# The first two chunks of w_out, and the first gate and up chunk, advanced side by side up to their last quarter

## The chip, the cores and the metric
The kernel runs on one core of one Trainium2 chip. The time is device microseconds of one execution (us); a matmul runs on the tensor engine (PE), with its weight loads recorded as PEld; DVE is the vector engine, ACT the scalar engine, POOL is GpSimd, SP the engine that issues most DMAs.

## What is computed
One residual block over x of shape (1, 256, 2048) in float32: an mLSTM branch and an S5 branch run on one normed input and are merged by two gates; then come an output projection, a gated feed-forward layer, and a last norm. The part around the change is

```python
merged = g[..., 0, :] * y_m + g[..., 1, :] * y_s
x = x + merged @ w_out                                   # 2048 x 2048
h2 = rms_norm(x, norm_ffn_g)
x = x + (silu(h2 @ w_ffn_gate) * (h2 @ w_ffn_up)) @ w_ffn_down   # hidden size 5632
return rms_norm(x, norm_final_g)
```

## The kernel before
All weights stream through the core once, as one list `blocks` (built near its end) of 512 KB pieces: 256 rows (two row tiles, "kts") by 512 columns. A matrix of 2048 rows has eight such pieces, kp 0 to 7, for each chunk n of 512 columns; out0.6 is here the piece kp 6 of chunk 0 of `w_out`, fg0.6 and fu0.6 the same of `w_ffn_gate` and `w_ffn_up`. `w_out` has four chunks, gate and up eleven each, and their chunks alternate: gate 0, up 0, gate 1, up 1, and so on.

Each piece takes the same way. SP issues its DMA into `raw` (L144). ACT casts it to `hi` (L156, the high part in a format that the PE takes at full rate), DVE computes `lo = raw - hi` (the TT helper, L94), and `o2_block` issues 12 matmuls of 128 rows by 512 columns (2 row tiles x 2 halves of the 256 sequence rows x 3 products: hi x hi, lo x hi, hi x lo), recorded on the helper's line L100. `raw`, `hi` and `lo` have three buffers each. A new DMA can start when the `lo` of three pieces before is done, and a new cast when the PE has finished the piece three before. From gate 0 on, every piece whose index in the list leaves 3 when divided by 4 (L140) takes its `raw` from another pool of 8 KB buffers instead, and so doesn't wait for those three. The loop at the end emits the DMA of piece i+5 and the split of piece i+2 before the matmuls of piece i.

The left operands come in quarters. `turn` (L969) takes chunk n of the merged branches (after the last piece of chunk n of `w_up_m`), transposes it, sends it through DRAM on POOL's queue (`groups_dma`, L281 out into `bounce`, L283 back, four DMAs each), and casts it to `mTh`/`mTl` (L979). Chunk 3 of it feeds pieces kp 6 and 7 of every chunk of `w_out`. In the same way `out_mm` loads a 256 x 512 part of x at its first piece (L998), and after its last piece it adds the accumulators (L1003), takes the squares (L1005) and queues `x1_T`: two transposes on DVE into `x1sd` (L274), two 256 KB DMAs out and eight 64 KB DMAs back on POOL's queue, then four `h2h` on ACT (L1027) and four `h2l` on DVE (L1028). Chunk 3 of these feeds pieces kp 6 and 7 of every chunk of gate and up; chunk 2 feeds kp 4 and 5. After chunk 3, DVE and ACT also compute the norm's factor `r2` (L244, L245). Accumulators are two PSUM tiles for a chunk, from a ring of four.

The written order is not the order that runs: the instructions of each engine are put in order when the program is built, by a scheduler that plays the program through (`schedule_with_timeline_sim=True`, L1351). In the kernel before it already starts out1.0 between out0.5 and out0.6, and runs fu0.0 between fg0.5 and fg0.6.

Of the kernel before, what the change touches and what calls it, by code (L numbers as in the profile page):

```python
# [15 lines left out]
ADD, SUB, MUL, MAX, MIN = ALU.add, ALU.subtract, ALU.mult, ALU.max, ALU.min  # L16
# [31 lines left out]
def block_kernel(ctx: ExitStack, tc: tile.TileContext, d, out):  # L48
# [14 lines left out]
    def nm(s):  # L63
        uid[0] += 1
        return f"{s}_{uid[0]}"

    def u8(shape, dt=F32, name="u"):
        return up.tile(shape, dt, tag="u8", name=nm(name), bufs=NU8)

    def u16(shape, dt=F32, name="U"):  # L70
        return up.tile(shape, dt, tag="u16", name=nm(name), bufs=NU16)
# [4 lines left out]
    def t2(shape=(P, 512), dt=F32, name="t"):  # L76
        return tp.tile(list(shape), dt, tag="t2k", name=nm(name), bufs=NT2)
# [4 lines left out]
    def acc_tile():  # L82
        return pp.tile([P, 512], F32, tag="acc", name=nm("acc"), bufs=4)
# [9 lines left out]
    def TT(o, a, b, op):  # L93
        return V.tensor_tensor(o, a, b, op=op)  # L94
# [4 lines left out]
    def mm(o, l, r, start, stop):  # L99
        return PE.matmul(o, l, r, start=start, stop=stop, skip_group_check=True)  # L100
# [25 lines left out]
    blocks = []  # L126

    def add_mat(name, nchunk, nkp, fn_maker, order=None):
        for n in order if order is not None else range(nchunk):
            for kp in range(nkp):  # L130
                blocks.append((d[name][n, kp], fn_maker, (n, kp)))
# [28 lines left out]
    def o2_block(acc, lhs, kts, hi, lo, first, last):  # L160
        n = len(kts)
        for q, kt in enumerate(kts):
            h = hi[:, q * 512 : (q + 1) * 512]
            l = lo[:, q * 512 : (q + 1) * 512]
            for tt in range(2):
                xh, xl = lhs(kt, tt)
                mm(acc[tt], xh, h, first and q == 0, False)
                mm(acc[tt], xh, l, False, False)
                mm(acc[tt], xl, h, False, last and q == n - 1)

    def lhs_of(hts, lts, per):
        def g(kt, tt):
            a, b = divmod(kt, per)
            s = slice(tt * 128, (tt + 1) * 128)
            return hts[a][:, b, s], lts[a][:, b, s]
        return g
# [619 lines left out]
    cur = {}  # L796
# [191 lines left out]
    def out_mm(i, nk, hi, lo):  # L988
        n, kp = nk
        if n == 0 and kp == 0:  # L990
            cur["x1"] = u16([P, 2, 2048], name="x1")
            cur["h2h"] = [u8([P, 8, 256], F32R, name="h2h") for _ in range(2)]
            cur["h2l"] = [u8([P, 8, 256], F32R, name="h2l") for _ in range(2)]
        if kp == 0:
            cur["acc"] = [acc_tile(), acc_tile()]
            cs = slice(n * 512, n * 512 + 512)
            with tc.issue_after(wdma[0]):
                nc.sync.dma_start(cur["x1"][:, :, cs], d["x"].rearrange("(a p) c -> p a c", p=P)[:, :, cs])  # L998
        o2_block(cur["acc"], lhs_of(cur["mTh"], cur["mTl"], 8), (2 * kp, 2 * kp + 1), hi, lo, kp == 0, kp == 7)
        if kp == 7:  # L1000
            for tt in range(2):
                o = cur["x1"][:, tt, n * 512 : n * 512 + 512]
                TT(o, cur["acc"][tt], o, ADD)  # L1003
                jk = t2()
                A.activation(jk, o, AF.Square, accum_out=ss2[:, tt, n : n + 1])  # L1005
            later(lambda: x1_T(n))

    def x1_T(n):
        sd = u8([P, 2, 1024], name="x1sd")
        st_ = sd[:, 0].rearrange("p (t j a c) -> p t j a c", j=4, t=2, a=4)  # L1010
        for tt in range(2):
            blocks_T(st_[:, tt], cur["x1"][:, tt, n * 512 : n * 512 + 512])

        def move():
            for tt in range(2):
                groups_dma(
                    sd[:, 1].rearrange("p (t i x) -> p t i x", t=2, i=4)[:, tt],
                    sd[:, 0].rearrange("p (t j x) -> p t j x", j=4, t=2)[:, tt],
                )
            later(split)  # L1020

        def split():
            d_ = sd[:, 1].rearrange("p (t i a c) -> p a (t i) c", i=4, t=2, a=4)
            for a in range(4):
                ct = 4 * n + a
                v = lambda h: h[ct // 8][:, ct % 8, :].rearrange("p (i c) -> p i c", c=32)
                A.activation(v(cur["h2h"]), d_[:, a], AF.Copy, scale=pvs("g2", ct))  # L1027
                STT(v(cur["h2l"]), d_[:, a], pvs("g2", ct), f(v(cur["h2h"])), MUL, SUB)  # L1028

        later(move, 0)  # L1030
        if n == 3:
            s = cp.tile([P, 2], F32, name="ssum2")
            V.tensor_reduce(s, ss2, mybir.AxisListType.X, ADD)
            TS(s, s, 1.0 / D, EPS, MUL, ADD)
            rstd(r2, s, "r2")
# [15 lines left out]
    def ffn_mm(which):  # L1051
        def fn(i, nk, hi, lo):
            n, kp = nk
            if kp == 0:
                cur[which] = [acc_tile(), acc_tile()]
            o2_block(cur[which], lhs_of(cur["h2h"], cur["h2l"], 8), (2 * kp, 2 * kp + 1), hi, lo, kp == 0, kp == 7)
            if kp == 7 and which == "fg":
                cur["t1"] = []
                for tt in range(2):
                    sg, t1 = t2(), t2()  # L1060
                    A.activation(sg, cur["fg"][tt], AF.Sigmoid, scale=r2[:, tt : tt + 1])
                    STT(t1, cur["fg"][tt], r2[:, tt : tt + 1], sg, MUL, MUL)
                    cur["t1"].append(t1)
            if kp == 7 and which == "fu":
                hh, ll = a_tiles(n)
                for tt in range(2):
                    STT(cur["t1"][tt], cur["fu"][tt], r2[:, tt : tt + 1], cur["t1"][tt], MUL, MUL)
                    turn(n, tt, cur["t1"][tt], hh, ll)

        return fn  # L1070
# [83 lines left out]
        blocks.insert(len(blocks) - GLU, (d["w_glu"][0, b], glu_mm, (0, b)))  # L1154
    add_mat("w_up_s", 4, 2, ups_mm)
    add_mat("w_up_m", 4, 4, upm_mm)
    add_mat("w_out", 4, 8, out_mm)
    fg, fu = ffn_mm("fg"), ffn_mm("fu")
    FFN0 = len(blocks)
    for n in range(11):  # L1160
        for kp in range(8):
            blocks.append((d["w_ffn_gate"][n, kp], fg, (n, kp)))
        for kp in range(8):
            blocks.append((d["w_ffn_up"][n, kp], fu, (n, kp)))
    add_mat("w_ffn_down", 4, 22, down_mm)

    laters = []
# [1 line left out]
    def later(fn, delay=1):  # L1169
        laters.append([delay, fn])  # L1170
# [63 lines left out]
    for i in range(len(blocks)):  # L1234
# [24 lines left out]
        hi, lo = splits.pop(i)  # L1259
# [95 lines left out]
```

## Time and profile before

| | |
|---|---|
| median of three runs | 1260.47 us (1258.69 to 1264.71) |
| the profiled execution | 1258.85 us, of which its span is 1257.1 us |
| PE busy | 1233.7 us (98% of the span) |
| DVE, ACT, POOL busy | 803.8, 604.0, 106.6 us |
| mean granted PE clock | 0.995 of full speed |
| DMA, mean over the span | 205 GB/s |
| chain that ended last | PE 85%, DVE 6%, DMA 5%, issue 2%, ACT 1% |

The times in the rows below count from the start of the span. The chain of waits follows the work that ended last back to what released it, so that a piece of another engine in it marks a place where the PE stood still or was close to it. The granted clock of a window is a share of full speed; 1.0 is 2.4 GHz and 0.5 is 1.2 GHz.

### The profile page before, as it was taken

To read this page: it belongs to the slowest core of one execution; us is meant where nothing else is said; L and a number is where in the kernel's file an instruction comes from. 1 tells how busy PE (TensorE), PEld (TensorE's weight loads), DVE (VectorE), ACT (ScalarE), POOL (GpSimd) and SP (SyncE) were. 2 spreads that over 40 slices of the span, in tenths; PEclk is the share of its full clock that TensorE was granted. 3 is DMA by queue.
4 is the path that set the end of the run, shared out by engine and by line. 5 is a ranking of instruction groups with operands and counts; after the bars stand their busy time and mean duration, and the time that the engine had idled before them with its cause. 6 is when DMAs were issued, how large, how long until landed. Compare 5 with 4: busy or idle time off the path is not lost.

```text
span 1257.1 us, 15683 instructions
## 1 busy us (share of the span) xinstructions
PE 1233.7 (98%) x5738; PEld 1015.3 (81%) x5738; DVE 803.8 (64%) x1162; ACT 604.0 (48%) x752; POOL 106.6 (8%) x199
## 2 busy tenths in 40 slices
PE   7999999999999999989999999999999999999997
PEld 7777888887788878868888888888888888888885
DVE  8779945999877856645556555555555554554544
ACT  7574554446654445444344444434444443444433
POOL 0000000000000522211101100110111010000000
PEclk9999999999999999989999999999999999999999
DMA  7645655554555977877667766555765686666443
GB/s 265 208 137 178 194 184 182 167 160 143 190 182 193 280 265 256 286 239 224 217 203 228 222 212 217 187 184 204 245 228 183 225 279 198 196 198 199 152 161 141
DMA packets 75597, 258.19 MB, mean 205 GB/s; under 512 B 10496, under 2 KB 11264, under 8 KB 75520
## 3 DMA queue, kind: packets, MB, share of 16 engines
q1 hardware_dynamic: 67616, 237.25, 58.1%
q0 software_dynamic: 7904, 19.94, 4.8%
q8 instruction: 45, 0.74, 0.2%
q14 instruction: 32, 0.26, 0.1%
HBM read 245.09 MB, written 12.06 MB: 205 GB/s over the span
## 4 chain that ended last, share of the span: by engine, by line
PE 85%; DVE 6%; DMA 5%; issue 2%; ACT 1%; ACTq 0%; SPq 0%; DVEq 0%
PE acc L100 80%; PE aux L100 4%; DMA raw<-in_w_out_dram 4%; DVE lo L94 3%; ACT hi L156 1%; DMA raw<-in_w_ffn_gate_dram 1%; DVE xcT L97 1%; DVE stm L94 0%; DVE bu L94 0%; DMA raw<-in_w_up_m_dram 0%; DVE x L94 0%; DVE gm L94 0%; DMA raw<-in_w_in_dram 0%; PE aux L774 0%; DVE h2l L97 0%
## 5 line engine op out<-in xcount | busy, mean ns | idle before, releaser
L94 DVE TENSOR_TENSOR lo<-raw,hi 128x1024 fp32r<-128x1024 f32 x427 | 521.0, 1221 | 403.6 <-ACT hi L156 403.0
L156 ACT CAST hi<-raw 128x1024 fp32r<-128x1024 f32 x427 | 449.1, 1053 | 577.5 <-PE acc L100 488.9
L100 PE MATMUL acc<-lo,h2h 128*128 128x512 f32 x704 | 275.2, 391 | 0.6 <-DVE lo L94 0.5
L100 PE MATMUL acc<-hi,h2l 128*128 128x512 f32 x704 | 274.2, 390 | 0.0
L100 PE MATMUL acc<-hi,h2h 128*128 128x512 f32 x704 | 246.8, 391 | 4.2 <-ACT hi L156 4.2
L100 PE MATMUL acc<-hi,aT 128*128 128x512 f32 x664 | 204.6, 389 | 0.0
L100 PEld LDWEIGHTS acc<-hi,h2h 128*128 128x128 f32 x704 | 132.5, 189 | 32.7 <-ACT hi L156 5.3
L100 PEld LDWEIGHTS acc<-lo,h2h 128*128 128x128 f32 x704 | 132.7, 189 | 29.6 <-DVE lo L94 2.1
L100 PE MATMUL acc<-lo,hTh 128*128 128x512 f32 x384 | 153.6, 400 | 1.3 <-DVE lo L94 1.2
L100 PEld LDWEIGHTS acc<-hi,h2l 128*128 128x128 f32 x704 | 132.8, 189 | 27.4
L100 PE MATMUL acc<-hi,hTl 128*128 128x512 f32 x384 | 150.4, 392 | 0.0
L100 PEld LDWEIGHTS acc<-hi,aT 128*128 128x128 f32 x664 | 124.7, 188 | 25.9
L100 PE MATMUL acc<-hi,hTh 128*128 128x512 f32 x384 | 139.4, 393 | 0.0
L100 PE MATMUL acc<-lo,aT 128*128 128x512 f32 x332 | 129.1, 389 | 0.0
L100 PEld LDWEIGHTS acc<-lo,hTh 128*128 128x128 f32 x384 | 72.1, 188 | 22.1 <-DVE lo L94 4.0
L100 PEld LDWEIGHTS acc<-hi,hTh 128*128 128x128 f32 x384 | 71.7, 188 | 16.7 <-issue 2.0
L100 PEld LDWEIGHTS acc<-hi,hTl 128*128 128x128 f32 x384 | 72.2, 188 | 14.6 <-issue 0.7
L281 POOL DMA_DIRECT2D bounce<-m x30 | 16.9, 565 | 690.5 <-DVE m L274 690.2
L100 PEld LDWEIGHTS acc<-lo,aT 128*128 128x128 f32 x332 | 62.3, 188 | 12.9
L283 POOL DMA_DIRECT2D m<-bounce x120 | 65.6, 554 | 43.1 <-DMA bounce<-m 28.2
L100 PE MATMUL acc<-lo,mTh 128*128 128x512 f32 x128 | 50.0, 392 | 0.0
L100 PE MATMUL acc<-hi,mTl 128*128 128x512 f32 x128 | 49.5, 389 | 0.0
(246 smaller groups left out, 1077.7 us busy)
## 6 DMA issues: line engine op xcount, KB each, us to landing
raw<-in_w_in_dram SPq DMA_DIRECT2D x104, 512.0 KB, 3.5
raw<-in_w_ffn_gate_dram SPq DMA_DIRECT2D x88, 512.0 KB, 3.7
raw<-in_w_ffn_up_dram SPq DMA_DIRECT2D x88, 512.0 KB, 4.2
raw<-in_w_ffn_down_dram SPq DMA_DIRECT2D x88, 512.0 KB, 3.5
raw<-in_w_out_dram SPq DMA_DIRECT2D x32, 512.0 KB, 5.0
raw<-in_w_up_m_dram SPq DMA_DIRECT2D x16, 512.0 KB, 3.6
bounce<-m POOLq DMA_DIRECT2D x30, 256.0 KB, 4.1
m<-bounce POOLq DMA_DIRECT2D x120, 64.0 KB, 4.2
```

The lines of the kernel that those rows point to most:

```text
L94: return V.tensor_tensor(o, a, b, op=op)
L97: return V.scalar_tensor_tensor(out=o, in0=a, scalar=s, in1=b, op0=op0, op1=op1, **kw)
L100: return PE.matmul(o, l, r, start=start, stop=stop, skip_group_check=True)
L156: A.copy(hi, raw)
L281: nc.gpsimd.dma_start(bounce, st_)
L283: nc.gpsimd.dma_start(dt_[32 * j : 32 * j + 32], bounce.rearrange("(i r) j x -> r i j x", i=4)[:, :, j])
```

## The change
The list of pieces is put in another order at two places. Chunks 0 and 1 of `w_out` run as out0.0 to out0.5, out1.0 to out1.5, out0.6, out0.7, out1.6, out1.7; chunks 2 and 3 follow as they were. Gate 0 and up 0 run as fg0.0 to fg0.5, fu0.0 to fu0.5, fg0.6, fg0.7, fu0.6, fu0.7; all later chunks are as they were. So that two chunks of `w_out` can be open at once, their accumulators are kept under a key of their own. Nothing else is edited.

```diff
@@ -992,15 +992,15 @@
         if kp == 0:
-            cur["acc"] = [acc_tile(), acc_tile()]
+            cur["out", n] = [acc_tile(), acc_tile()]
...
-        o2_block(cur["acc"], lhs_of(cur["mTh"], cur["mTl"], 8), (2 * kp, 2 * kp + 1), hi, lo, kp == 0, kp == 7)
+        o2_block(cur["out", n], lhs_of(cur["mTh"], cur["mTl"], 8), (2 * kp, 2 * kp + 1), hi, lo, kp == 0, kp == 7)
...
-                TT(o, cur["acc"][tt], o, ADD)
+                TT(o, cur["out", n][tt], o, ADD)
@@ -1154,14 +1154,20 @@
-    add_mat("w_out", 4, 8, out_mm)
+
+    SPLIT = 6
+    for ms, a, b in (((0, 1), 0, SPLIT), ((0, 1), SPLIT, 8), ((2, 3), 0, 8)):
+        for m in ms:
+            for kp in range(a, b):
+                blocks.append((d["w_out"][m, kp], out_mm, (m, kp)))
     fg, fu = ffn_mm("fg"), ffn_mm("fu")
     FFN0 = len(blocks)
     for n in range(11):
-        for kp in range(8):
-            blocks.append((d["w_ffn_gate"][n, kp], fg, (n, kp)))
-        for kp in range(8):
-            blocks.append((d["w_ffn_up"][n, kp], fu, (n, kp)))
+        for a, b in ((0, SPLIT), (SPLIT, 8)) if n == 0 else ((0, 8),):
+            for kp in range(a, b):
+                blocks.append((d["w_ffn_gate"][n, kp], fg, (n, kp)))
+            for kp in range(a, b):
+                blocks.append((d["w_ffn_up"][n, kp], fu, (n, kp)))
```

The first place is on the PE where out0.5 ends. In the kernel before, `acc_4033` and `acc_4034` are chunk 0 and `acc_4204`, `acc_4205` chunk 1; `hi_4104` is out0.5, `hi_4122` out0.6, `hi_4158` out1.0.

```order
L100 MATMUL acc_4034<-lo_4105,mTh_3643 128x512
L100 MATMUL acc_4034<-hi_4104,mTl_3645 128x512
L100 MATMUL acc_4204<-hi_4158,mTh_3642 128x512
L100 MATMUL acc_4205<-hi_4158,mTh_3642 128x512
L100 MATMUL acc_4033<-hi_4122,mTh_3643 128x512
L100 MATMUL acc_4033<-lo_4123,mTh_3643 128x512
L100 MATMUL acc_4204<-lo_4159,mTh_3642 128x512
```

In the changed kernel, at the same place, `acc_4162` and `acc_4163` are chunk 1 and `hi_4122`, the next buffer to be filled after `hi_4104`, is out1.0.

```order
L100 MATMUL acc_4034<-lo_4105,mTh_3643 128x512
L100 MATMUL acc_4034<-hi_4104,mTl_3645 128x512
L100 MATMUL acc_4162<-hi_4122,mTh_3642 128x512
L100 MATMUL acc_4163<-hi_4122,mTh_3642 128x512
L100 MATMUL acc_4162<-lo_4123,mTh_3642 128x512
L100 MATMUL acc_4162<-hi_4122,mTl_3644 128x512
```

Out1.0 was the third piece to be loaded and cast after out0.5, and is now the first; the PE took it at this place before, too.

The second place is the gate. SP issues, from fg0.4 (`raw_4702`) on, before the change:

```order
L144 DMA raw_4702<-in_w_ffn_gate_dram 128x1024
L144 DMA raw_4788<-in_w_ffn_gate_dram 128x1024
L144 DMA raw_4868<-in_w_ffn_up_dram 128x1024
L144 DMA raw_4950<-in_w_ffn_up_dram 128x1024
L144 DMA raw_5022<-in_w_ffn_gate_dram 128x1024
L144 DMA raw_5117<-in_w_ffn_gate_dram 128x1024
L144 DMA raw_4726<-in_w_ffn_gate_dram 128x1024
L144 DMA raw_4758<-in_w_ffn_gate_dram 128x1024
L144 DMA raw_4806<-in_w_ffn_up_dram 128x1024
```

and after it:

```order
L144 DMA raw_4702<-in_w_ffn_gate_dram 128x1024
L144 DMA raw_4788<-in_w_ffn_up_dram 128x1024
L144 DMA raw_4868<-in_w_ffn_up_dram 128x1024
L144 DMA raw_4942<-in_w_ffn_up_dram 128x1024
L144 DMA raw_5022<-in_w_ffn_gate_dram 128x1024
L144 DMA raw_5117<-in_w_ffn_gate_dram 128x1024
L144 DMA raw_4726<-in_w_ffn_gate_dram 128x1024
L144 DMA raw_4758<-in_w_ffn_up_dram 128x1024
L144 DMA raw_4806<-in_w_ffn_up_dram 128x1024
```

In both, five transfers into the other pool stand between fg0.4 and fg0.5 (`raw_4726`); they were fg0.7, fu0.3, fu0.7, fg1.3, fg1.7 and are now fu0.1, fu0.5, fu0.7, fg1.3, fg1.7. Behind fg0.5 follow fg0.6 and fu0.0 before, and fu0.0 and fu0.2 now. ACT fills the `hi` of `raw_4726`, `raw_4758`, `raw_4788` and `raw_4806` in this order in both kernels, as `hi_4808`, `hi_4834`, `hi_4852` and `hi_4870`. On the PE, behind fg0.5, before:

```order
L100 MATMUL acc_4733<-lo_4809,h2h_4030 128x512
L100 MATMUL acc_4733<-hi_4808,h2l_4032 128x512
L100 MATMUL acc_4918<-hi_4870,h2h_4029 128x512
L100 MATMUL acc_4919<-hi_4870,h2h_4029 128x512
L100 MATMUL acc_4918<-lo_4871,h2h_4029 128x512
```

and now, where `acc_4874` and `acc_4875` are up 0:

```order
L100 MATMUL acc_4733<-lo_4809,h2h_4030 128x512
L100 MATMUL acc_4733<-hi_4808,h2l_4032 128x512
L100 MATMUL acc_4874<-hi_4834,h2h_4029 128x512
L100 MATMUL acc_4875<-hi_4834,h2h_4029 128x512
L100 MATMUL acc_4874<-lo_4835,h2h_4029 128x512
```

The PE took fu0.0 from the fourth buffer filled (`hi_4870`) and takes it now from the second (`hi_4834`), which is the next behind fg0.5's.

The third place is on ACT, where the four `h2h` of a chunk of `w_out` stand between the casts. Chunk 2's (`x1sd_4571`) stood behind the casts of fg0.0 (`raw_4622`) and fg0.1 (`raw_4648`):

```order
L156 CAST hi_4668<-raw_4604 128x1024
L156 CAST hi_4686<-raw_4622 128x1024
L156 CAST hi_4704<-raw_4648 128x1024
L1027 ACTIVATE h2h_4030<-x1sd_4571,pv 128x256 x4
L156 CAST hi_4728<-raw_4666 128x1024
```

In the changed kernel the same rows read:

```order
L156 CAST hi_4668<-raw_4604 128x1024
L1027 ACTIVATE h2h_4030<-x1sd_4571,pv 128x256 x4
L156 CAST hi_4686<-raw_4622 128x1024
L156 CAST hi_4704<-raw_4648 128x1024
L156 CAST hi_4728<-raw_4666 128x1024
```

Chunk 0's, which stood between the casts of out2.1 and out2.2, now stand between those of out2.5 (`raw_4366`) and out2.6 (`raw_4390`):

```order
L156 CAST hi_4430<-raw_4330 128x1024
L156 CAST hi_4448<-raw_4366 128x1024
L1027 ACTIVATE h2h_4029<-x1sd_4327,pv 128x256 x4
L156 CAST hi_4474<-raw_4390 128x1024
L156 CAST hi_4492<-raw_4428 128x1024
```

On DVE the same holds of `h2l` and `lo`. At the ends of chunks 2 and 3 of `w_out` DVE now has the two additions (L1003) and the two transposes (L274) together ahead of the `lo` of out3.2 and fg0.2, where before `h2l` and that `lo` lay among them. On POOL the move of chunk 1 stands behind the whole move of chunk 0, as before.

## Rows read from the trace of the kernel before

**Rows 1.** Windows: length, PE, PEld, DVE, ACT, POOL (instructions), clock, DMA share, GB/s

```profile
440.00:450.00 10.00, 8.48 (x38) 6.66 (x36) 5.26 (x6) 5.18 (x6) 4.38 (x8) 1.00 0.95 341
...
530.00:540.00 10.00, 6.89 (x27) 4.93 (x26) 3.04 (x6) 2.64 (x4) 4.21 (x8) 0.89 0.97 353
540.00:550.00 10.00, 8.35 (x27) 5.85 (x27) 4.67 (x7) 3.88 (x7) 0.15 (x1) 0.77 0.76 236
```

**Rows 2.** Timeline of PE, first pieces of w_out: start, us, instruction [idle before <-releaser]

```profile
431.59 0.62 PE L100 MATMUL acc<-hi,mTh 128*128 128x512 f32 x2
...
434.31 0.62 PE L100 MATMUL acc<-hi,mTh 128*128 128x512 f32 x2
...
447.68 0.39 PE L100 MATMUL acc<-hi,mTl 128*128 128x512 f32 x1
...
449.59 1.02 PE L100 MATMUL acc<-hi,mTh 128*128 128x512 f32 x3 [1.52 <-ACT hi L156]
...
451.41 0.40 PE L100 MATMUL acc<-lo,mTh 128*128 128x512 f32 x1
```

**Rows 3.** Timeline of ACT, same stretch

```profile
444.63 1.05 ACT L156 CAST hi<-raw 128x1024 fp32r<-128x1024 f32 x1 [2.64 <-DMA raw<-in_w_out_dram]
...
448.49 1.04 ACT L156 CAST hi<-raw 128x1024 fp32r<-128x1024 f32 x1 [0.69 <-DMA raw<-in_w_out_dram]
```

**Rows 4.** Chain of waits in order of time: start, us, what

```profile
442.75 5.64 DMA raw<-in_w_out_dram
...
525.99 1.15 DVE lo L94
...
527.15 9.94 DMA raw<-in_w_ffn_gate_dram
...
546.57 701.64 PE acc L100 x3094
```

**Rows 5.** Timeline of PE, end of fg0.5 and fu0.0

```profile
538.28 1.22 PE L100 MATMUL acc<-hi,h2h 128*128 128x512 f32 x2 [3.07 <-ACT hi L156]
...
541.41 0.63 PE L100 MATMUL acc<-hi,h2h 128*128 128x512 f32 x1
...
543.55 0.63 PE L100 MATMUL acc<-hi,h2l 128*128 128x512 f32 x1
...
545.31 0.74 PE L100 MATMUL acc<-hi,h2h 128*128 128x512 f32 x2 [1.13 <-ACT hi L156]
...
546.57 0.50 PE L100 MATMUL acc<-lo,h2h 128*128 128x512 f32 x1 [0.52 <-DVE lo L94]
```

**Rows 6.** Timeline of ACT, gate 0

```profile
518.26 1.05 ACT L156 CAST hi<-raw 128x1024 fp32r<-128x1024 f32 x1 [2.29 <-DMA raw<-in_w_ffn_gate_dram]
...
521.85 1.70 ACT L1027 ACTIVATE h2h<-x1sd,pv 128x256 fp32r<-128x256 f32 x4
...
537.19 1.04 ACT L156 CAST hi<-raw 128x1024 fp32r<-128x1024 f32 x1 [7.16 <-DMA raw<-in_w_ffn_gate_dram]
...
544.22 1.04 ACT L156 CAST hi<-raw 128x1024 fp32r<-128x1024 f32 x1 [3.80 <-PE acc L100]
```

**Rows 7.** DMA issues from 524.0 to 526.9: op xcount, KB each, median us to landing

```profile
raw<-in_w_ffn_gate_dram SPq DMA_DIRECT2D x3, 512.0 KB, 8.3
raw<-in_w_ffn_up_dram SPq DMA_DIRECT2D x2, 512.0 KB, 6.1
```

**Rows 8.** Timeline of POOL: the moves of chunks 2 and 3

```profile
512.54 4.37 POOL L283 DMA_DIRECT2D x1sd<-bounce  x8 [6.15 <-DMA bounce<-x1sd]
...
528.04 1.15 POOL L281 DMA_DIRECT2D bounce<-x1sd  x2 [11.13 <-DVE x1sd L274]
```

**Rows 9.** DMA issues from 527.9 to 529.4, and from 512.4 to 517

```profile
bounce<-x1sd POOLq DMA_DIRECT2D x2, 256.0 KB, 7.5
...
x1sd<-bounce POOLq DMA_DIRECT2D x8, 64.0 KB, 4.6
```

**Rows 10.** Timeline of DVE, end of chunk 2

```profile
504.25 1.29 DVE L274 STREAM_TRANSPOSE x1sd<-x 128x512 f32<-128x512 f32 x2
```

## The prediction

> **What bounds the kernel now.** The page's busy table comes first: PE 98% of the span, so the rest is 23 us in all, and a change of order can only win what of it lies at the places it touches. The chain of waits then says where those are. From 546.57 it is one row of 701.64 us of PE to the end [rows 4]: nothing behind that point is ever late, so every us that PE reaches it earlier comes off the end, and nothing behind it can be won. Between the first piece of `w_out` and there the chain leaves PE at two places. By count there is a measure for both: twelve matmuls take 434.31 - 431.59 = 2.72 us [rows 2], one 0.227.
>
> Place A is the end of out0.5. PE starts its last matmul at 447.68 and the next, out1.0's, at 449.59, 1.52 us of it idle, released by ACT's cast [rows 2]. The seventh matmul behind 447.68 should start at 447.68 + 7 x 0.227 = 449.27 and starts at 451.41: **A costs 2.1 us**. The cast ran at 448.49, behind a DMA that was issued at 442.75 and took 5.64 us [rows 3, 4]. Out1.0 was the third piece in the queue though the PE takes it first; the first of the three was cast at 444.63 [rows 3].
>
> Place B is gate 0, with two stops. At fg0.5 PE waits 3.07 us for a cast that ran at 537.19, when fg0.5's DMA, issued at 527.15, had landed after 9.94 us [rows 4 to 6]. Its issue waited for the `lo` at 525.99 [rows 4]; its slowness is the five transfers of the other pool issued just ahead, 6 to 8 us each [rows 7]. Once PE had stood, the granted clock was 0.89 and 0.77 in two windows of 10 us [rows 1], that is half speed (1.2 GHz) for (0.11 + 0.23) x 10 / 0.5 = 6.8 us, and the eleven steps from 538.28 to 543.55 took 5.27 us in place of 2.49. **The stop at fg0.5 costs 3.2 + 2.8 = 6.0 us.** The second stop is fu0.0: due at 543.55 + 0.23, its third matmul due at 544.23, it starts that at 546.57 [rows 5], and the clock is not quite back, so **fu0.0 costs 2.4 us**. ACT's cast for it, at 544.22, waited 3.80 us for PE and no DMA [rows 6]: three `hi` buffers were held by fg0.5, fg0.6 and fg0.7, cast ahead of fu0.0, while PE wants fu0.0 before two of them.
>
> So the order in which pieces are loaded and the order in which PE takes them disagree at A and at fu0.0, and agree at fg0.5. This is what the change touches.
>
> **The change part by part.** No instruction of the matrix work is added or taken out: the same pieces, casts, `lo` and matmuls.
>
> *Place A.* Out1.0 takes the position of the piece whose cast ran at 444.63 to 445.68 [rows 3]; its `lo`, 1.2 us more, is done by 447, and PE wants it at 447.9. Both waits go: **-2.1**. Next late would be out0.6, which needs the last quarter of `mTh`, but now runs 6 pieces, 16.3 us, later; that covers it many times over.
>
> *fu0.0.* It is cast right behind fg0.5, into a buffer that fg0.3 left long ago. Its transfer is the one behind fg0.5's in the queue, whose cast before ran straight after the row at 537.19 [rows 6] while PE is busy with fg0.5 until 543.8. The waits go. But the first two or three matmuls still run at 1.2 GHz, since the clock came back only near 537.8 + 6.8 = 544.6: 0.4 us stay. **-2.0**.
>
> *fg0.5.* The same five transfers still stand ahead of it. PE and the chain of `raw` buffers both come 2.1 us earlier, as the last point before this chain where a cast waits for PE (near 458) moves with PE. So its wait and its half clock stay: **0**, and I look for reasons why it should move. DVE's `lo` of fg0.2 (released fg0.5's issue) stands behind two additions and two transposes now, no longer behind `h2l`: 1.3 us more of transposes (a pair [rows 10]), 0.9 less of `h2l`. The moves of chunk 3 (two DMAs out, then eight back [rows 8]) now start about 2 us earlier, so that some of the eight may fall into fg0.5's own transfer. Eight of 64 KB are 512 KB, as much as one piece; by the five of that burst one takes 6.1 / 5 to 8.3 / 5, 1.2 to 1.7 us [rows 7]. Bounds 0 and +1.6; since only the tail of fg0.5's transfer can meet them, **+0.3**.
>
> Here a page of the Trainium skill bears, "DMA: Bandwidth & Descriptors", section "Queues, rings and completion order". First the row: POOL's two transfers out were issued at 528.04, after fg0.5's, and took 7.5 us [rows 8, 9], landing near 535.5, before fg0.5's at 537.09. The rule says that each DMA engine takes turns between the queues that have work; the trace agrees. By that rule an earlier start on POOL's queue takes its share from fg0.5 in any case, and the term would be the upper bound, 1.6; first come, first served would give 0.
>
> *`h2h` ahead of casts.* Chunk 2's four (1.70 us [rows 6]) now stand ahead of fg0.0's cast, chunk 0's ahead of out2.6's. From the end of chunk 2's transposes, 505.5 [rows 10], to its last transfer back, 516.9 + 4.6 = 521.5 at the latest [rows 8, 9], a move takes 16 us. With PE on its new course (out0.0 at 431.59, 2.72 a piece), chunk 0 is complete after 14 pieces at 469.8, its additions and transposes (2.7 us) end at 472.5, its move by 488.5; `h2h` ends at 490.2 and out2.6 is cast by 491.3. PE wants out2.6 after 22 pieces, at 491.4. Likewise chunk 2 is complete at 496.9, its transposes at 499.6, the move at 515.6, `h2h` at 517.3, fg0.0 cast by 518.4, wanted at 518.6. Both just fit for `hi`; `lo` follows 1.2 us behind a cast and PE wants it 0.45 behind the start of the piece, so up to 0.8 us is lost at each. Bounds 0 and +1.6, and I take **+0.3**, as a move of 16 us is the longest that the rows allow.
>
> Behind gate 0 the order is as it was, and up 0's end covers the end of gate 0 with two pieces, 5.4 us.
>
> *Sum.* 1258.85, the profiled execution, - 2.1 - 2.0 + 0.3 + 0.3 = 1255.35. That execution lies 1.6 below the median of the three; halfway, 0.8, is added: **1256.1**.
>
> **Rivals.**
>
> *The stop at fg0.5 falls as well.* If the earlier end of `h2l` lets `lo` of fg0.2 and with it fg0.5's issue come some 1.6 us sooner (that `lo` then follows its own cast and the additions at once), PE's wait is 1.5 us, and no fall of the clock followed the wait of 1.52 us at A (the clock there read 1.00 [rows 1]). Then 1.6 + 2.8 more go: about 1251.5. Against: five transfers of 512 KB stand ahead of it, whenever it is issued.
>
> *The gain at A is eaten at fg0.5.* If the burst there is set by the DMAs alone and doesn't move with PE, PE comes 2.1 us earlier and waits 2.1 longer: 1258.85 - 2.0 + 0.6 + 0.8 = 1258.2. For it: DMA share 0.97 in that window [rows 1]. Against: each transfer into `raw` waits for a `lo`, which waits for a cast, which last waited for PE.
>
> *A new stop at out2.6: slower.* Chunks 0 and 1 end 5.4 us apart and not 24, so that chunk 0's move meets chunk 1's load of x and a queue of weights without slack, and ACT is shut to all casts until it has landed. PE's wait grows one for one with a move beyond 16.1 us. With the half clock, which followed a wait of 3.07 us and not one of 1.52, it makes the kernel slower than before from a move of 18 to 19 us on. At 20 us PE stands 3.9 + 0.8, and the half clock costs 2.8 as at fg0.5: 7.5 us, less the 0.3 counted: 1256.1 + 7.2 = 1263.3. Against: the longest move in the trace is 16, and the second chunk's move waits its turn on POOL.
>
> *The change does nothing*, since the scheduler had already moved out1.0 and fu0.0: 1259 to 1260.5. Against: their buffers and transfers do change place.
>
> **How the numbers follow.** Forecast 0.56, with its own range of 1253.5 to 1258 from the bounds above; fg0.5 also won 0.16; A eaten 0.13; out2.6 0.10; nothing 0.05. The range for 8 in 10 reaches down to 1250.5 (the first rival and its spread) and up to 1261, leaving out most of the out2.6 case and a little of the first. 0.5%, about what a measurement of this kernel can tell, is 6.3 us: faster means below 1254.2, which takes the first rival and about a fifth of the forecast, 0.15 + 0.11 = 0.26; slower means above 1266.8, a worse out2.6, 0.04; the rest, 0.70, is within.
>
> **What would show it.** In the trace after: no wait of PE on ACT at the start of out1.0, and none at fu0.0; fg0.5 with a DMA of 9 to 11 us, a wait near 3 us and half clock for some 7 us; then PE unbroken to the end, from about 543 instead of 546.57. The rivals show as a clock of 1.00 through gate 0; as a longer wait at fg0.5 (5 us); as a wait of PE at out2.6 or fg0.0 behind `h2h`. I am wrong if moves of x1 take much over 16 us, or if the burst at fg0.5 breaks up.

## The result

The changed kernel takes 1253.73 us (median of 6, 1251.19 to 1254.60) against 1260.46 before: 0.9939 of the time, 95% interval 0.9921 to 0.9958. A second set of runs gave 1254.81 against 1260.53, 0.9958 (0.9941 to 0.9975). The forecast was 1256.1 in a range of 1250.5 to 1261.0. The profiled execution took 1254.09 us, its span 1252.2.

The page of the changed kernel, its span and its busy times:

```profile
span 1252.2 us, 15688 instructions
...
PE 1231.2 (98%) x5738; PEld 1015.3 (81%) x5738; DVE 804.8 (64%) x1162; ACT 604.5 (48%) x752; POOL 106.7 (9%) x199
```

The engines carry out as many matmuls, weight loads, casts and transposes as before. What changed is where PE stands. The chain of waits of the changed kernel, in order of time (start, us, what), as [rows 4]:

```profile
436.11 6.38 DMA raw<-in_w_out_dram
...
444.95 57.17 PE acc L100 x251
...
505.97 8.03 DMA raw<-in_w_out_dram
...
524.04 10.86 DMA raw<-in_w_ffn_gate_dram
...
537.36 705.97 PE acc L100 x3106
```

PE now runs through to the end from 537.36, where it was 546.57. That is not 9 us won: the last piece of the chain begins at fg0.5, not at fu0.0, with some half-speed matmuls behind it. The timeline of PE after the change has these waits and no other between the first piece of `w_out` and the end of up 0 (compare [rows 2, 5]):

```profile
444.95 0.50 PE L100 MATMUL acc<-lo,mTh 128*128 128x512 f32 x1 [0.53 <-DVE lo L94]
...
533.08 0.39 PE L100 MATMUL acc<-hi,h2l 128*128 128x512 f32 x1
536.10 0.73 PE L100 MATMUL acc<-hi,h2h 128*128 128x512 f32 x2 [2.63 <-ACT hi L156]
537.36 0.50 PE L100 MATMUL acc<-lo,h2h 128*128 128x512 f32 x1 [0.52 <-DVE lo L94]
```

The wait at out1.0 (1.52 us before) is gone, the one at fu0.0 (1.13 + 0.52) is gone, and the stop at fg0.5 has stayed, 2.63 us and not 3.07. The windows (columns as in [rows 1]) show the half clock shorter:

```profile
530.00:540.00 10.00, 6.84 (x26) 4.96 (x25) 2.59 (x3) 3.04 (x3) 4.37 (x8) 0.91 1.03 356
540.00:550.00 10.00, 10.00 (x42) 8.13 (x41) 6.26 (x8) 5.03 (x8) 0.00 (x0) 0.92 0.83 268
```

(0.09 + 0.08) x 10 / 0.5 = 3.4 us at 1.2 GHz, where before it was 6.8.

To compare kernels I take one measure from each trace: the time between the starts of two matmuls less 0.2267 us for each step between them (2.72 / 12, [rows 2]); what is left is what PE lost. From the first matmul of `w_out` to the first of gate 0 are 384 steps, gate 0 and up 0 are the next 192. Behind them nothing is lost but 0.4 to 1.1 us near 720 us in four of the traces (the second of before, gate's part alone, and both with single pieces moved); the column "in all" holds it. Each row of losses is read from one execution. Those of the gate's part alone and of the old list with transfers in order took 1.9 and 2.9 us more than the median of their kernel, and that of the single pieces with chunk 0's move put off 2.2 us less; the others lie within 1.7 us of it. All kernels of this study:

| kernel | lost in w_out | lost in gate 0 and up 0 | lost in all | time over before (95%) |
|---|---|---|---|---|
| before, first and second profile | 2.6, 5.7 | 8.8, 6.9 | 11.3, 13.0 | 1 |
| changed, first and second profile | 0.9, 0.0 | 5.4, 5.4 | 6.2, 5.3 | 0.9939, 0.9958 |
| w_out's part alone | 0.3 | 8.4 | 8.7 | 0.9983 (0.9972 to 0.9995) |
| gate's part alone | 4.2 | 4.9 | 9.7 | 0.9972 (0.9959 to 0.9986) |
| single pieces moved | 3.3 | 6.9 | 11.2 | 0.9994 (0.9982 to 1.0007) |
| the same, chunk 0's move put off | 2.4 | 4.1 | 7.6 | 0.9978 (0.9964 to 0.9991) |
| before, transfers in order | 2.8 | 6.6 | 9.4 | 0.9977 (0.9962 to 0.9991) |
| w_out's part, transfers in order | 0.1 | 2.2 | 2.3 | 0.9924 (0.9909 to 0.9939) |
| gate's part, transfers in order | 2.6 | 0.4 | 3.0 | 0.9945 (0.9930 to 0.9959) |
| changed, four transfers ahead of fg0.5 | 0.0 | 2.2 | 2.2 | 0.9936 (0.9921 to 0.9950) |
| changed, three transfers ahead of fg0.5 | 0.2 | 1.6 | 1.8 | 0.9922 (0.9908 to 0.9936) |
| changed, transfers in order | 0.0 | 1.0 | 1.0 | **0.9916** (0.9902 to 0.9931) |

### The profile page after: what moved, and what is told of

It is laid out like the page before. It is cut to its first block, busy times and chain, and to the rows that moved or that the text cites. A ratio compares the mean times of both kernels' runs of the same rounds, so it can differ in the third digit from the quotient of the medians.

```text
span 1252.2 us, 15688 instructions
## 1 busy us (share of the span) xinstructions
PE 1231.2 (98%) x5738; PEld 1015.3 (81%) x5738; DVE 804.8 (64%) x1162; ACT 604.5 (48%) x752; POOL 106.7 (9%) x199
## 4 chain that ended last, share of the span: by engine, by line
PE 90%; DVE 4%; DMA 3%; issue 1%; ACT 1%; POOL 0%; ACTq 0%; SPq 0%; DVEq 0%
PE acc L100 85%; PE aux L100 4%; DVE lo L94 2%; DMA raw<-in_w_out_dram 1%; DMA raw<-in_w_ffn_gate_dram 1%; DVE xcT L97 1%; ACT hi L156 1%; DVE stm L94 1%; DVE bu L94 0%; DMA m<-bounce 0%; DMA raw<-in_w_in_dram 0%; POOL m L283 0%; PE aux L774 0%; DVE xcT L94 0%; DVE x L94 0%
```

## The experiments

### Each part alone

W_out's part alone keeps the old loop of gate and up; the gate's part alone keeps `add_mat("w_out", 4, 8, out_mm)`.

```diff
-        for a, b in ((0, SPLIT), (SPLIT, 8)) if n == 0 else ((0, 8),):
-            for kp in range(a, b):
-                blocks.append((d["w_ffn_gate"][n, kp], fg, (n, kp)))
...
+        for kp in range(8):
+            blocks.append((d["w_ffn_gate"][n, kp], fg, (n, kp)))
```

> Only w_out's chunks 0 and 1 run side by side; gate 0 and up 0 stand as in the kernel before. My theory (each place pays for itself, the stops at gate 0 move with PE): the wait at out1.0 goes, 1.7 us as in the trace of the changed kernel, and both stops at gate 0 keep their 8.7 us: 0.9986 of the time before, about 1258.7. Rival (the gain at w_out is eaten at gate 0, because the transfers there don't move with PE): 1260.5, with a wait at fg0.5 longer by 1.7 us, near 4.8. Second rival (the earlier h2h of chunk 2 empties ACT and DVE and so eases fg0.5 too): 1256 or less, with a wait at fg0.5 under 2.8 us.

> Only gate 0 and up 0 run side by side; w_out stands as in the kernel before, with its wait at out1.0. My theory: the second stop (fu0.0) goes and the half clock is shorter, 3.4 us as in the changed kernel: 0.9973, about 1257.1; the wait at fg0.5 stays near 3 us. Rival (the shorter half clock belongs to w_out's part): only 2.0 us, 0.9984, 1258.5, with half clock for 6 to 7 us. Rival (the whole gain is here): 5.1 us, 0.996, 1255.4.

Both came out at the forecast of the first theory: 0.9983 and 0.9972, together 0.9955 where the whole gave 0.9939 and 0.9958. The places pay for themselves. With w_out's part alone the stop at fg0.5 is longer than in either trace of before, and the wait at fu0.0 is there:

```profile
536.98 0.87 PE L100 MATMUL acc<-hi,h2h 128*128 128x512 f32 x2 [3.84 <-ACT hi L156]
...
543.14 0.73 PE L100 MATMUL acc<-hi,h2h 128*128 128x512 f32 x2 [1.13 <-ACT hi L156]
```

3.84 against 3.07 in the first trace of before: 0.8 us of what `w_out` won may have been given back at fg0.5, a part of the prediction's second rival, and hidden in the sum by a half clock of 3.4 us here, too. One trace doesn't show it for certain, since the same wait was 1.96 us in the second trace of before, where the PE came to fg0.5 3.2 us later.

### Only the two pieces moved

```diff
+    for m, kp in [(0, k) for k in range(6)] + [(1, 0), (0, 6), (0, 7)] + [(1, k) for k in range(1, 8)] + [(m, k) for m in (2, 3) for k in range(8)]:
+        blocks.append((d["w_out"][m, kp], out_mm, (m, kp)))
...
+        if n == 0:
+            gu.insert(6, gu.pop(8))
```

> The list of before with two single pieces moved: out1.0 ahead of out0.6, fu0.0 ahead of fg0.6. Nothing else runs side by side, and chunk 0's move stays early. My theory (what counts is that pieces are loaded in the order in which PE takes them): as fast as the changed kernel within 1.5 us, 0.994 to 0.9955, no wait at out1.0 and none at fu0.0. Rival (the last quarters must be put off by six pieces, since chunk 3 of mT and of h2 come too late): out0.6 or fg0.6 wait, and at most 2 us of the gain are left, 0.9985 to 1.0.

My theory fell as it was put. The waits at out1.0 and at fu0.0 are gone, as they must be if the order of loading made them, yet nothing is won: 0.9994. That lies in the range of the rival, but its cause is not there either, since neither out0.6 nor fg0.6 waits. The loss moved. On ACT of this kernel, behind the cast of out2.0:

```profile
470.16 1.05 ACT L156 CAST hi<-raw 128x1024 fp32r<-128x1024 f32 x1 [0.80 <-PE acc L100]
474.93 1.71 ACT L1027 ACTIVATE h2h<-x1sd,pv 128x256 fp32r<-128x256 f32 x4 [3.72 <-DMA x1sd<-bounce]
476.55 1.98 ACT L156 CAST hi<-raw 128x1024 fp32r<-128x1024 f32 x2
```

ACT stands 3.72 us before chunk 0's `h2h`, with the casts of out2.1 and out2.2 behind it, and PE then waits for `lo` in out2.1, out3.0 and out3.6, 3.3 us lost in `w_out` altogether. This is the mechanism of the rival that I had priced for out2.6, at another piece. In the changed kernel chunk 0 is complete five pieces' time later than here, and the scheduler puts its `h2h` where ACT stands 0.88 us and PE not at all:

```profile
486.48 1.71 ACT L1027 ACTIVATE h2h<-x1sd,pv 128x256 fp32r<-128x256 f32 x4 [0.88 <-DMA x1sd<-bounce]
489.35 2.25 ACT L156 CAST hi<-raw 128x1024 fp32r<-128x1024 f32 x2 [1.16 <-DMA raw<-in_w_out_dram]
```

To see whether that early move was the cause, it was put off:

```diff
-            later(lambda: x1_T(n))
+            later(lambda: x1_T(n), 9 if n == 0 else 1)
```

> The list with the two single pieces moved, and the transposes and the move of w_out's chunk 0 put off by eight pieces, so that its four h2h on ACT stand with chunk 1's. With the early move ACT stood 3.7 us before h2h of chunk 0 with casts behind it, and w_out lost 3.3 us in all. My theory (an early move takes the slack that the piece moved had won): under 1 us lost in w_out, 2 to 3 us less than with the early move, 0.997 to 0.998. Rival (the slack goes to the transfers of x and of the weights themselves): 2 to 3 us still lost, 0.999 to 1.0.

0.9978, the ratio that I expected, but not for the reason: `w_out` still lost 2.4 us, so the rival holds there. Putting the move off won back 0.9 us of the 3.3. ACT no longer waits for a move, but as long as before for transfers of `w_out`: from 455 to 525 us it waits 19.5 us for them here, 20.6 with the early move, 25.2 and 20.7 in the two traces of before, and only 9.6 and 9.9 in those of the changed kernel. PE waits at out2.6 and out3.6. Much of the gain over the early move in these two traces is a missing half clock at gate 0 (4.1 lost, not 6.9). What takes the slack inside `w_out` when PE is 2 us ahead is thus settled in part only: the wait behind `h2h` is shown, the rest lies with the transfers, which run further ahead where two chunks go side by side, and why they do wasn't pulled apart.

### The transfers ahead of fg0.5

```diff
-            wdma[0] = nc.sync.dma_start(raw, blocks[i][0]).ins
+            with tc.issue_after(wdma[0]) if FFN0 + 4 <= i < len(blocks) - NTAIL - 4 and i % 4 == 3 else ExitStack():
+                wdma[0] = nc.sync.dma_start(raw, blocks[i][0]).ins
```

> The changed kernel, with the transfers into the other pool issued in the order of the list (none runs ahead of the piece before it). My theory (the five transfers ahead of it make fg0.5 late): fg0.5's transfer takes 4 to 6 us, no wait and no half clock at gate 0, 5.3 us less than the changed kernel: 0.990, about 1248. Rival (the DMAs are at their limit there with or without the five, the moves of x1 doing it): a wait of 1 to 3 us stays, 1251 to 1254. Rival (what runs ahead there is needed later): new waits of PE in gate 1 and behind, 1255 or more.

1248.61 us, 0.9916. Fg0.5's DMA now takes 5 us, ACT casts it 7 us earlier, and PE goes through gate 0 at a clock of 1.00 (ACT, then PE, then a window of this kernel):

```profile
528.09 1.05 ACT L157 CAST hi<-raw 128x1024 fp32r<-128x1024 f32 x1 [1.87 <-DMA raw<-in_w_ffn_gate_dram]
```

```profile
542.61 0.50 PE L100 MATMUL acc<-lo,h2h 128*128 128x512 f32 x1 [0.53 <-DVE lo L94]
```

```profile
530.00:540.00 10.00, 10.00 (x46) 8.29 (x45) 3.66 (x6) 3.45 (x6) 0.08 (x1) 1.00 0.85 249
```

No new wait came up in gate 1 or behind. The wait left, 0.53 us, is at fu0.2, whose cast stands behind the `h2h` of chunk 3 on ACT. (The lines of this kernel's code are one further down than before.)

The number of transfers ahead was then varied: with `FFN0 + 20` and `FFN0 + 16` in place of `FFN0 + 4`, four and three of them run ahead; the list and PE's order are the same.

> The changed kernel with four transfers of the other pool ahead of fg0.5's in place of five (from the fifth on they are issued in the order of the list). In two profiles of the changed kernel PE stood 2.8 and 3.4 us at fg0.5 and half clock took about 2 more. If the five are the cause, one less takes one transfer's time, 1.2 to 1.7 us, off the wait: 1.1 to 2.2 us; the half clock may stay: 1.5 us (up to 3.5 where it goes) less than the changed kernel, 0.9925 to 0.9945. Rival (the limit is what all queues move there): the wait stays above 2.5 us.

> The same with three ahead of fg0.5's transfer. By the same count the wait at fg0.5 is 0 to 1 us, no half clock follows, and the time is within 1 us of the kernel with none ahead: 0.9915 to 0.9925. Rival: the wait falls less than 1.2 us per transfer taken away, and 2 us or more stay.

0.9936 (0.9921 to 0.9950) and 0.9922 (0.9908 to 0.9936). The first matmul of fg0.5 with four, then with three ahead:

```profile
534.02 0.73 PE L100 MATMUL acc<-hi,h2h 128*128 128x512 f32 x2 [1.10 <-ACT hi L157]
```

```profile
533.19 0.73 PE L100 MATMUL acc<-hi,h2h 128*128 128x512 f32 x2 [0.47 <-ACT hi L157]
```

With five it waits 2.63 and, in the second profile, 3.23; with four 1.10, with three 0.47, with none it doesn't. Fg0.5's own transfer, in the second profile of the changed kernel (chain of waits) and then with four, three and none ahead (DMA issues):

```profile
522.96 11.72 DMA raw<-in_w_ffn_gate_dram
```

```profile
raw<-in_w_ffn_gate_dram SPq DMA_DIRECT2D x1, 512.0 KB, 9.8
raw<-in_w_ffn_gate_dram SPq DMA_DIRECT2D x1, 512.0 KB, 8.8
raw<-in_w_ffn_gate_dram SPq DMA_DIRECT2D x1, 512.0 KB, 5.2
```

The mean with five is (10.86 + 11.72) / 2 = 11.3, so (11.3 - 5.2) / 5 = 1.2 us for each 512 KB ahead of it, at the low end of the 1.2 to 1.7 that the prediction had read from [rows 7]. Chunk 3's move out of `x1sd` stands ahead of fg0.5's transfer in all of them, also where PE doesn't wait. So the five are the cause, and the first one taken off is worth most, since no half clock followed the shorter waits: gate 0 and up 0 lose 5.4 us with five and 2.2 with four.

### The order of the list once fg0.5 comes in time

> The kernel before, its list untouched, with the transfers into the other pool issued in the order of the list. In its own trace w_out lost 2.6 us against PE at its full rate and gate 0 with up 0 lost 8.8. My theory (the stop at fg0.5 is the five transfers, the one at fu0.0 the order of casts): the stop at fg0.5 goes with its half clock, the waits at out1.0 and fu0.0 stay, 2.6 + 2.4 us lost, 6.3 less: 0.995, about 1253, and 4 to 4.5 us behind the changed kernel with the same edit. Rival (once fg0.5 is there in time, casts run ahead and fu0.0 doesn't wait either): 8.8 less, 0.993, 1250.5.

> Only w_out's chunks 0 and 1 side by side, gate 0 and up 0 as before the change, and the transfers into the other pool in the order of the list. If the split of gate 0 and up 0 is worth something by itself once fg0.5 comes in time: 1 to 2.4 us slower than the changed kernel with the same edit, 0.9925 to 0.9935, with a wait at fu0.0 or fg0.6. If it only mended the order of casts that the burst had spoiled: the same time, 0.9916 within 0.0005.

> Gate 0 and up 0 side by side, w_out as before the change, transfers into the other pool in the order of the list. If the places add up: no stop at gate 0, and w_out loses 2.6 to 4.2 us at out1.0 as in the two traces with that list: 2 to 3.5 us slower than the kernel with both parts and the same edit, 0.9935 to 0.9945. Rival (w_out's part is worth nothing once gate 0 is in order, since the later PE finds its pieces there): 0.9916.

The old list with the transfers in order reached only 0.9977, and neither theory nor rival had its size right: the stop at fg0.5 went, and fu0.0's grew to 3.88 us with a half clock behind it (PE, then ACT, of the kernel before with that edit):

```profile
544.45 0.73 PE L100 MATMUL acc<-hi,h2h 128*128 128x512 f32 x2 [3.88 <-ACT hi L157]
```

```profile
533.20 1.05 ACT L157 CAST hi<-raw 128x1024 fp32r<-128x1024 f32 x1 [0.60 <-DMA raw<-in_w_ffn_gate_dram]
539.02 1.05 ACT L157 CAST hi<-raw 128x1024 fp32r<-128x1024 f32 x1 [4.77 <-DMA raw<-in_w_ffn_gate_dram]
540.66 1.04 ACT L157 CAST hi<-raw 128x1024 fp32r<-128x1024 f32 x1 [0.59 <-PE acc L100]
543.36 1.04 ACT L157 CAST hi<-raw 128x1024 fp32r<-128x1024 f32 x1 [1.65 <-DMA raw<-in_w_ffn_up_dram]
```

These are fg0.5, fg0.6, fg0.7 and fu0.0. PE has fu0.0 next behind fg0.5, ended by 540.6, and must wait until two pieces that it wants later are loaded and cast. Loaded and cast second, in fg0.6's place, fu0.0 would have been cast by 540.1, in time; and fg0.6 could not stand in for it, since chunk 3's `h2h`, which it needs, began at 545.74. So this stop is the disagreement of the two orders; the transfers, for which ACT waits 4.77 and 1.65 us, set its length.

With w_out's part and transfers in order the scheduler left fg0.6 ahead of fu0.0, so that the orders agree again, and PE waits for something else, chunk 3 of `h2`:

```profile
537.50 0.50 PE L100 MATMUL acc<-hi,h2h 128*128 128x512 f32 x1 [1.90 <-ACT h2h L1028]
```

1.9 us; the gate's part takes it away, 0.9924 against 0.9916 (the intervals overlap, so that the times don't show a gain; the traces lose 2.3 and 1.0). And with the gate's part alone `w_out` loses its 2.6 us, 0.9945. So where the stop at fg0.5 is gone each part is still worth something by itself, but the two no longer add up: from 0.9977 with neither, the gate's part wins 0.0032, w_out's 0.0053, and both together 0.0061 and not 0.0085. They share the stop at fu0.0: the gate's part removes it, and with w_out's part the scheduler happened to leave fg0.6 ahead of fu0.0, so that it didn't arise.

### Both kernels once more

> The changed kernel once more, unedited, for a second profile and more runs beside the one before. The two traces differ by 5.1 us, the two medians by 6.7. If the traces are typical: 0.9959 of the time before, within 0.001. If the half clock at gate 0 (6.8 us long in the trace before, 3.4 in that after) comes out by chance, the second profile may show 6.8 again, with 1.4 us more lost there.

> The kernel before once more, unedited, for a second profile. If the first profile was typical: 11.3 us lost by PE from the first piece of w_out on, 2.6 in w_out and 8.8 in gate 0 with up 0, with a half clock of 6.8 us. If the half clock's length comes out by chance, 3.4 us of it may be seen, and a loss near 10 us. The ratio is 1.0 within 0.002.

0.9958 (0.9941 to 0.9975) and 0.9998 (0.9983 to 1.0013). The changed kernel's second profile loses 5.3 us, the first 6.2. The first profile of the kernel before was less typical than I took it for: the second lost 13.0 us. There PE waits 2.55 us at out1.0 and only 1.96 at fg0.5, and a half clock follows at out1.0, too (PE at both places, then a window):

```profile
450.90 1.32 PE L100 MATMUL acc<-hi,mTh 128*128 128x512 f32 x3 [2.55 <-ACT hi L156]
...
540.34 0.73 PE L100 MATMUL acc<-hi,h2h 128*128 128x512 f32 x2 [1.96 <-ACT hi L156]
```

```profile
450.00:460.00 10.00, 9.10 (x33) 7.24 (x34) 4.69 (x6) 3.38 (x5) 0.00 (x0) 0.83 0.44 145
```

The mean of the two pairs of profiles, 12.2 - 5.8 = 6.4 us, agrees with the two differences of medians, 6.7 and 5.7.

## Why the prediction was right, and where it was off

**What bounds the kernel** held: all that was won or lost, but for the 0.4 to 1.1 us near 720 us, lies between the first piece of `w_out` and the end of up 0, and passes to the end one for one. The losses in the table differ as the spans of the profiled executions do, to within 1.4 us (the old list with transfers in order aside, see below).

**Place A, -2.1**: right in kind; the size depends on the trace. The traces lost 2.6 and 5.7 in `w_out` before, 0.9 and 0.0 after. In the first pair that is 1.7 won (the 0.9 left is a wait for `lo` at 444.95, ahead of out1.0, which the second trace doesn't have), by the means of the pairs 3.7. The second trace of before shows that I had the milder form: a longer wait at out1.0 brings a half clock.

**fu0.0, -2.0**: the wait is gone. That its cause is the order of casts was read from a row in which ACT waited for PE [rows 6]; the old list with transfers in order, where the stop stays and grows to 3.88 us without the one at fg0.5, and the kernel with single pieces moved, where it is gone, bear this out.

**fg0.5, "0", with +0.3 for the moves of chunk 3**: against the trace that the sum started from, this is the term that was mis-sized. Gate 0 and up 0 lost 8.8 us there and 5.4 after, 3.4 less, where the sum had 2.0 - 0.3 = 1.7 less. The wait itself hardly changed (3.07 and 1.96 before, 2.63 and 3.23 after). Between the first traces, two things that I had weighed both happened and about cancelled. Fg0.5's DMA was issued at 524.04 and not at 527.15, 3.1 us sooner while PE was 1.8 sooner (533.08 for 534.83), so by 1.4 against PE; that is the first rival's cause. And it took 10.86 us (11.72 in the second trace) in place of 9.94 (9.27 in the second trace of before), 0.9 to 1.8 more than 9.94, about my upper bound of 1.6. The moves had been issued ahead of it this time, at 522.37 (POOL), and took 7.9 us (DMA issues from 520 to 523.9):

```profile
522.37 1.15 POOL L281 DMA_DIRECT2D bounce<-x1sd  x2 [14.84 <-DVE x1sd L274]
```

```profile
bounce<-x1sd POOLq DMA_DIRECT2D x2, 256.0 KB, 7.9
```

The rule of the Trainium skill's page "DMA: Bandwidth & Descriptors" (section "Queues, rings and completion order": each DMA engine takes turns between the queues that have work) made that upper bound the term, and the rows agree with it better than with the 0.3 that I took; they don't show how much of the 0.9 to 1.8 is the moves'. What I had not foreseen is the length of the half clock, 3.4 us and not 6.8, worth (6.8 - 3.4) / 2 = 1.7 us. It is the whole difference of the term. I had carried the 6.8 of one profile over as if it belonged to the stop. It doesn't: the second trace of before has half clocks of 3.4 us only, and against that trace gate 0 and up 0 won 1.5 us, close to the sum's 1.7. So the 1.7 us is luck of the first pair of traces and not a gain of the change. Over both pairs `w_out` won 3.7 us where the sum had 2.1 less the 0.3 for `h2h`, and the gate 2.4 where it had 1.7: the forecast was too small, by half clocks that come and go from execution to execution.

**h2h ahead of casts, +0.3**: nothing was lost at out2.6 or fg0.0. A move took less than my 16 us: chunk 0's `h2h` began at 486.48, 13.5 us behind its transposes.

**From the profile to the median, +0.8**: the sum for the profiled execution was 1255.35 and that execution took 1254.09. The correction went the wrong way by 1.2: the changed kernel's median lies 0.4 below its profiled execution. In the second set it lies 1.7 above, so that neither sign could be known from one profile.

**The rivals**: none came out as the whole, but one of them lives in another kernel: ACT shut to casts by an early `h2h` where single pieces were moved (of the 3.3 us lost in `w_out`, putting the move off won back 0.9). The gain eaten at fg0.5 may show in w_out's part alone (0.8 us). The prediction's line for "faster", 1254.2, to which it gave 0.26, lies between the two medians of the changed kernel (1253.73 and 1254.81): the gain is about 0.5%.

**What is open**: why the half clock lasts 3.4 us in one execution and 6.8 in another. The trace of the old list with transfers in order reaches `w_out` at 434.30 where the others reach it at 431.6 to 432.4; that comes from its start, far ahead of the change, where PE waits 1.52 us and then runs at half clock for (1 - 0.83) x 10 / 0.5 = 3.4 us (PE, then a window):

```profile
20.16 1.22 PE L100 MATMUL acc<-hTh,lo 128*128 128x256 f32 x4 [1.52 <-DVE lo L94]
```

```profile
20.00:30.00 10.00, 9.84 (x69) 9.84 (x70) 9.71 (x26) 6.30 (x13) 0.00 (x0) 0.83 0.54 164
```

From its hundredth matmul to `w_out` that trace stays 2.7 us behind the first trace of before. Its execution, 1260.28, is the slowest of the kernel's runs.

## What to carry to other kernels

Where a scheduler reorders the matmuls, see whether the pieces are still loaded and cast in the order in which the PE takes them: a piece that is pulled ahead while its cast stands behind two others makes a stop, which shows as a cast that waits for PE while PE waits for that cast. Before the order of the work is changed, count the transfers that stand ahead of the late one: taking five of them out of the way, on top of the change, won 3 to 5 us (from 0.9939 and 0.9958 to 0.9916) where the change itself won 5 to 8, and without the change about 3 (0.9977), since the stop at fu0.0 grew in its place. A short stop can cost nearly double where the clock falls behind it (3.2 us of stop and 2.8 of half clock at fg0.5 before), so shortening a stop may pay more than its length. And one profile is one execution: two of the same kernel differed by 1.7 us here in what PE lost, and by more at each single place, so take a second before a term of the sum is read from it.

## What the runs showed of the hardware

After single waits of PE of 2.1 to 3.9 us the granted clock fell to half (1.2 GHz) and stayed there for 3.4 us in most profiles and 6.8 in two (the first of before, and the one with single pieces moved), for the same kernel one or the other: (1 - 0.83) x 10 / 0.5 = 3.4 in the second profile of before at out1.0. After most single waits of 0.5 to 1.9 us it stayed at 1.00. It fell twice behind shorter waits that stood close together: behind 0.31 and 1.52 us at 17.43 and 20.16 (the old list with transfers in order), and behind 1.96, 0.53, 1.13 and 0.53 us between 540.34 and 546.56 (the second profile of before, whose window from 540 to 550 reads 0.85); behind 1.32, 0.53 and 1.33 us between 536.7 and 544.6 it didn't fall (single pieces with chunk 0's move put off). So a wait of 1.5 us is no sure sign that the clock stays up.

A transfer of 512 KB took 5.2 us with none of the burst ahead of it on its own queue, 8.8 with three, 9.8 with four and 10.9 and 11.7 with five. In the window of the stop, 530 to 540 us, the DMAs' busy share was 0.97 before, 1.03 after, and 0.85 with none of the burst ahead.
